# Key normalisation as one reciprocal on one side, the triangular inverse tied to its data, and a new order of lanes in the RWKV-7 stage of a hybrid decoder layer

## The chip, the cores and the metric

The kernel is one program for one core of a Trainium2 chip. The metric is device time of one execution in microseconds (us), the median of several executions. "Before" is the kernel without the change, "after" the kernel with it.

## The reference

One layer of a hybrid decoder on an input of 1 x 1024 x 1024 in float32: norm, one combined input projection, an RWKV-7 branch and an S5 branch side by side, gates, a merge, an output projection, and a gated convolutional FFN. What the change touches is the RWKV-7 branch, with 8 heads of 64 channels over 1024 positions:

```python
kk = (k * k_k).reshape(hs)
kk = kk / jnp.maximum(jnp.linalg.norm(kk, axis=-1, keepdims=True), 1e-12)
k = k * (1.0 + (a - 1.0) * k_a)
...
y = wkv7_scan(rh, decay.reshape(hs), kh, vh, -kk, kk * ah)

def step(S, inp):                      # in wkv7_scan, over the positions
    r_t, w_t, k_t, v_t, a_t, b_t = inp
    sa = jnp.einsum('bhij,bhj->bhi', S, a_t)
    S = (S * w_t[:, :, None, :] + sa[..., None] * b_t[:, :, None, :]
         + v_t[..., None] * k_t[:, :, None, :])
    return S, jnp.einsum('bhij,bhj->bhi', S, r_t)
```

Here a_t is -kk and b_t is kk times a, both with the normalised key. In the state's update they occur only as a product, an a of one position with a b of another of the same head. Behind the scan each head's output is normalised (mean and variance over 64 channels), scaled, and a bonus is added.

## The kernel before

All large products are fp32 made of three products of split operands (L172 to L174, high by high, high by low, low by high; each 128x512). Their results go to PSUM, an activation or an add takes them out, and ACT and DVE split weights and data into halves (L156, L157). TensorE is in use nearly throughout.

The RWKV stage is cut into four units i = 0..3: a group of four heads (i%2) on half of the sequence (i//2). Each unit has two halves u = 0, 1 of two heads each, 128 channels on the partitions and 512 positions on the free axis. A unit goes through these steps:

- **Front** (`rwkv_front`, once per u). Loads key, rate and decay (tiles `ld`), squares the key on ACT (L668), sums it per head on PE (L672), which gives 8 sums per partition, and takes the inverse root with eleven small DVE instructions (`rsqrt`, L136 to L141, 128x8 each, or 128x8 in integers). The decay goes through a running sum (L679, DVE) and two exponentials (L681, L682, ACT). The inverse norm is spread over 512 columns (L687, ACT, into a part of `gr`) and transposed on PE into `kb` (L689), after which four 512-wide DVE instructions (L690, L691, L693, L694) make the a side `ar` and the b side `bk`. GpSimd (POOL) makes the other halves (L665, L666, L678, L692, L695, L696) and copies the last decay of each chunk into `pt` (L683). Then come the Gram products of 64 positions (L706) with masks on DVE (L709) into `gr`, their store to DRAM (`md`, L714), and the bonus (L718).
- **Inverse** (`rwkv_inv`). The 32x32 unit triangular blocks of `gr` come back from `md` in another layout (`mt`, L756). The solution `x` starts as the identity (L757, an ACT copy of a constant), and 31 steps of two DVE instructions (L763, L765) eliminate row after row. `x` goes to DRAM (`xd`, L768) and back into `gr` (L775). POOL issues all these transfers.
- **Nat** (`rwkv_nat`, per u). Transposes of `bk` (L736), their copies `bkn` on ACT (L739), transposes of v (L745) and a copy to `V` (L747).
- **Level** (`rwkv_level`). DVE transposes the inverted blocks (L787, into a tile of the `ld` ring), small products join two blocks to 64 (L794, L802).
- **Chain** (`rwkv_chain`): 8 chunks in sequence, each L835 (state times a), a copy `p` and two scalings `spt` = S by `pt` (L840) on ACT, L844, a copy `U` on DVE (L846), L852 and L854, and the new state S (L856, DVE). `chain_v` (L817 to L821) is the part that needs no state.
- **Out** (`rwkv_out`): the norm of `yn` on DVE (L869 to L879), transposes of the result on PE (L885), scale (L887), two additions (L892), and a store.

**What sets the order.** The order of PE's instructions is written out by `drive`. It runs lanes, which are Python generators. A lane yields a cost and a delay: the cost is added to a virtual clock, and the lane may go on once the clock has passed the delay. At each point the first lane in the list that is ready goes on. When none is, or when the lanes have used up a credit, a piece of background work (the large gate, merge and projection products) is placed. So the constants T_... decide how many large products stand between a step and its successor, and the list decides who goes first. The other engines' instructions are ordered by a scheduler from priorities and its own simulation; each engine then runs strictly in its order. `prep_lane(u)` holds front and inverse, `chain_lane` nat, level, chain and out. The front of unit i+1 may start when nat of unit i is done.

Of the kernel before, what the change touches and what calls it, by code (L numbers as in the profile page):

```python
# [9 lines left out]
F32 = mybir.dt.float32  # L10
# [61 lines left out]
class Kern:  # L72
# [572 lines left out]
    def rwkv_front(self, d, u):  # L645
# [11 lines left out]
        def c64(x):  # L657
            return x.rearrange("p (c t) -> p c t", t=64)
# [15 lines left out]
        sv = self.small.tile([128, 8], F32, tag="sv", name=self.nm("sv"), bufs=2)  # L674
        V.tensor_scalar(sv, st.rearrange("p a b -> p (a b)"), 1e-24, None, ALU.max)
        y = self.rsqrt(sv, 8, "pr")

        G.tensor_scalar(tz, tz, 1.0, 1.0, ALU.add, ALU.mult)  # L678
# [4 lines left out]
        G.tensor_copy(d["pt"][:, :, u], pe[:, :, 64])  # L683
# [6 lines left out]
        V.scalar_tensor_tensor(kk, k, self.vec("k_k", p), kb, ALU.mult, ALU.mult)  # L690
        V.scalar_tensor_tensor(ar0, c64(kk), -1.0, pe[:, :, 0:64], ALU.mult, ALU.mult)  # L691
        G.tensor_tensor(ar1, c64(r), pe[:, :, 1:65], ALU.mult)  # L692
        V.scalar_tensor_tensor(kk, ta, 1.0, kk, ALU.add, ALU.mult)  # L693
        V.scalar_tensor_tensor(bk0, c64(kk), 0.5, c64(tz), ALU.mult, ALU.mult)  # L694
# [29 lines left out]
    def rwkv_nat(self, d):  # L724
# [6 lines left out]
        for u in range(2):  # L731
# [8 lines left out]
            yield 1.0, 0.3  # L740
# [6 lines left out]
            A.copy(d["V"][:, :, u], ps)  # L747
            yield 1.0, 0.8

    def rwkv_inv(self, d):  # L750
# [6 lines left out]
        A.copy(x, self.cst("xinit").rearrange("p (s t) -> p s t", t=32).unsqueeze(1).to_broadcast([128, 2, 8, 32]))  # L757
        mt = mt.rearrange("p u (q t) -> p u q t", t=32)
        for q in range(31):
# [17 lines left out]
    def rwkv_level(self, d):  # L777
# [5 lines left out]
        xz = self.tg("ld", NLD).rearrange("p (u c t) -> p u c t", u=2, t=32)  # L783
# [78 lines left out]
    def rwkv_out(self, d):  # L862
# [17 lines left out]
        yield 0, T_LN  # L880
# [813 lines left out]
    def front_half(self):  # L1694
# [35 lines left out]
        with tc.tile_pool(name="rk", bufs=1) as self.rk, tc.tile_pool(name="evb", bufs=NEV) as self.evp, \  # L1730
# [4 lines left out]
            self.nat = self.prep = -1  # L1735
# [33 lines left out]
    def chain_lane(self, mg):  # L1769
        for i, d in enumerate(self.ds):  # L1770
# [20 lines left out]
T_LD, T_LT = 9.0, 3.0  # L1791
NEVA = 4
T_KN, T_BK, T_GR, T_INV, T_LV, T_CH, T_LN = 5.0, 9.0, 2.5, 36.0, 1.0, 0.8, 11.0
# [87 lines left out]
```

## Time and profile before

| | us |
|---|---|
| median of 3 runs | 1615.97 |
| lowest and highest run | 1611.21, 1623.19 |
| profiled execution, whole | 1613.51 |
| its span in the trace | 1611.7 |
| PE busy in the span | 1508.9 (94%) |
| mean granted TensorE clock | 0.962 of full speed |

The span is the time from the first to the last instruction of the profiled execution; the remaining 1.8 us lie around it. The RWKV stage takes about 285 to 715 us of it. "Clock" is the share of full TensorE speed that was granted: a stretch of 6 us with a clock of 0.50 ran at half speed throughout.

### The profile page before, as it was taken

The numbers are of one execution on the slowest core, as the hardware profiler recorded it, in microseconds if no ns is written. First come the engines' busy times: TensorE is split into PE (matmuls) and PEld (weight loads), VectorE is DVE, ScalarE is ACT, GpSimd is POOL, SyncE is SP. The second block draws the span as 40 slices with busy tenths as digits, with TensorE's granted clock in tenths as the row PEclk, the third lists the DMA queues.
The fourth block names the chain that finished last, engine by engine and source line by source line (L and its number), as shares of the span: only waits on it lengthen the run. The fifth ranks groups of instructions, "written<-read, shape, count | busy, mean of one in ns | idle before, by whom it ended". The sixth has DMA issues, their size and how long they took to land. (4 is left out here: it accounts for less than half of the span.)

```text
span 1611.7 us, 26125 instructions
## 1 busy us (share of the span) xinstructions
PE 1508.9 (94%) x10028; PEld 1207.6 (75%) x10028; DVE 1126.7 (70%) x2039; ACT 696.8 (43%) x1109; POOL 155.0 (10%) x226
## 2 busy tenths in 40 slices
PE   5899899898999999889998999999999999999995
PEld 4688787686776776667866888788888887788784
DVE  5798774565365555865668579977777776788677
ACT  4345552224233344554443445554444444443451
POOL 2100001314123142010000000000000000000000
PEclk9799999999999999989988999999999999999997
DMA  5244334243352353552574453322222224963622
GB/s 178 63 140 142 98 113 169 65 136 117 106 153 94 97 171 107 171 156 93 190 223 156 144 190 125 124 79 83 90 89 78 78 87 142 321 215 106 229 84 104
DMA packets 133420, 213.84 MB, mean 133 GB/s; under 512 B 38656, under 2 KB 44800, under 8 KB 133296
## 3 DMA queue, kind: packets, MB, share of 16 engines
q1 hardware_dynamic: 124208, 188.32, 35.5%
q0 software_dynamic: 7936, 21.77, 4.6%
q10 hardware_dynamic: 1152, 2.10, 0.3%
q8 instruction: 78, 1.28, 0.3%
q14 instruction: 46, 0.38, 0.1%
HBM read 156.56 MB, written 53.48 MB: 130 GB/s over the span
## 5 line engine op out<-in xcount | busy, mean ns | idle before, releaser
L172 PE MATMUL gm<-hh,wh 128*128 128x512 f32 x688 | 299.6, 436 | 6.5 <-ACT hh L226 3.3
L173 PE MATMUL gm<-hl,wh 128*128 128x512 f32 x688 | 279.1, 406 | 5.4 <-DVE hl L227 4.5
L174 PE MATMUL gm<-hh,wl 128*128 128x512 f32 x688 | 276.6, 402 | 0.0
L156 ACT CAST wh<-wf 128x512 fp32r<-128x512 f32 x179 | 110.7, 620 | 196.7 <-PE gm L173 108.5
L157 DVE TENSOR_TENSOR wl<-wf,wh 128x512 fp32r<-128x512 f32 x179 | 124.8, 698 | 100.7 <-ACT wh L156 97.5
L172 PEld LDWEIGHTS gm<-hh,wh 128*128 128x128 f32 x688 | 134.0, 195 | 45.2 <-ACT hh L226 5.6
L173 PEld LDWEIGHTS gm<-hl,wh 128*128 128x128 f32 x688 | 134.2, 195 | 32.4 <-DVE hl L227 7.3
L174 PEld LDWEIGHTS gm<-hh,wl 128*128 128x128 f32 x688 | 134.1, 195 | 30.0
L1504 PE MATMUL d<-xl,wh 128*128 128x512 f32 x308 | 121.1, 393 | 3.3 <-DVE xl L227 3.3
L1503 PE MATMUL d<-xh,wh 128*128 128x512 f32 x308 | 120.8, 392 | 2.1 <-ACT xh L226 2.1
L1505 PE MATMUL d<-xh,wl 128*128 128x512 f32 x308 | 120.5, 391 | 0.0
L1329 PE MATMUL rp<-t,h 128*128 128x512 f32 x216 | 84.4, 391 | 1.9 <-ACT p L1343 1.9
L1331 PE MATMUL rp<-t,l 128*128 128x512 f32 x216 | 84.2, 390 | 0.5 <-DVE l L227 0.5
L1330 PE MATMUL rp<-t,h 128*128 128x512 f32 x216 | 84.1, 389 | 0.0
L1504 PEld LDWEIGHTS d<-xl,wh 128*128 128x128 f32 x308 | 58.1, 189 | 16.8 <-DVE xl L227 4.9
L1503 PEld LDWEIGHTS d<-xh,wh 128*128 128x128 f32 x308 | 58.2, 189 | 14.7 <-ACT xh L226 2.5
L1505 PEld LDWEIGHTS d<-xh,wl 128*128 128x128 f32 x308 | 58.2, 189 | 12.2
L226 ACT CAST h<-r 128x1024 fp32r<-128x1024 f32 x34 | 35.8, 1054 | 61.4 <-PE rp L1330 29.6
L227 DVE TENSOR_TENSOR l<-r,h 128x1024 fp32r<-128x1024 f32 x34 | 41.6, 1225 | 29.5 <-ACT h L226 28.0
L1350 DVE SCALAR_TENSOR_TENSOR y<-zv,vecs,y 128x1023 f32<-128x1023 f32 (+1 forms) x36 | 46.1, 1280 | 8.6 <-ACT y L1348 8.6
L1329 PEld LDWEIGHTS rp<-t,h 128*128 128x128 f32 x216 | 40.5, 188 | 11.4 <-ACT p L1343 2.7
L1331 PEld LDWEIGHTS rp<-t,l 128*128 128x128 f32 x216 | 40.5, 188 | 9.3 <-DVE l L227 1.0
(437 smaller groups left out, 3364.1 us busy)
## 6 DMA issues: line engine op xcount, KB each, us to landing
r<-in_w_up_dram SPq DMA_DIRECT2D x36, 512.0 KB, 3.2
wf<-in_w_in_dram SPq DMA_DIRECT2D x68, 256.0 KB, 2.9
st<-in_w_down_dram SPq DMA_DIRECT2D x55, 256.0 KB, 4.3
st<-ACT SPq DMA_DIRECT2D x44, 256.0 KB, 4.4
wf<-in_w_up_dram SPq DMA_DIRECT2D x36, 256.0 KB, 2.8
ACT<-y POOLq DMA_DIRECT2D x18, 512.0 KB, 2.9
GT<-ev SPq DMA_DIRECT2D x32, 256.0 KB, 2.3
wf<-in_w_br_dram SPq DMA_DIRECT2D x32, 256.0 KB, 3.1
```

The costliest lines, as they stand in the source:

```text
L156: nc.scalar.copy(h[:, :n], f[:, :n])
L157: nc.vector.tensor_tensor(l[:, :n], f[:, :n], h[:, :n].bitcast(F32), ALU.subtract)
L172: mm(ps, a, xh[k], start=k == 0, stop=False)
L173: mm(ps, a, xl[k], start=False, stop=False)
L174: mm(ps, b, xh[k], start=False, stop=k == n - 1)
L1329: mm(ps, wh[:, c], xh, start=first and k == 0, stop=False, skip_group_check=True)
L1330: mm(ps, wh[:, c], xl, start=False, stop=False, skip_group_check=True)
L1331: mm(ps, wl[:, c], xh, start=False, stop=k == 3, skip_group_check=True)
L1350: V.scalar_tensor_tensor(y[:, lag:], z[:, 0:1024 - lag], self.vec(nme, i), y[:, lag:], ALU.mult, ALU.add)
L1503: mm(ps, wh[:, c], xh[:, x], start=start, stop=False, skip_group_check=True)
L1504: mm(ps, wh[:, c], xl[:, x], start=False, stop=False, skip_group_check=True)
L1505: mm(ps, wl[:, c], xh[:, x], start=False, stop=stop, skip_group_check=True)
```

## The change

- **Norm on one side.** The root is gone. `sv` is the sum, bounded below, and one reciprocal of it (128x8) goes to the b side alone; the a side gets key by `k_k` by decay without a norm. Since a and b are only ever multiplied with each other within a head, this needs the reciprocal of the squared norm that belongs to b's position; the a side's own norm is carried by nothing else. Three of the four 512-wide DVE instructions now stand ahead of the reciprocal, and only one, the last product of the b side, needs `kb`.
- **Small moves.** The addition of 1 to the decay's tanh moves from POOL in the front to POOL in the input stage, ahead of that tile's store. The `pt` copy moves from POOL to ACT.
- **Inverse.** The ACT copy of the constant is gone. The first elimination step (row 0, whose multiplier is the constant's first column) is folded with it into three DVE instructions: two products of 128x256 and one addition of 128x512. They read `mt`, so `x` is not written before `mt` is there. The other 30 steps stay.
- **Level's tile.** The tile for the transposed blocks is taken in nat, and a copy of two columns from nat's last PSUM tile into it (ACT) ties the DVE transposes behind nat.
- **Lanes.** The front lanes stand ahead of the chain in the list. Out is a lane of its own at the end of the list, and chain i waits until out i-1 has been placed.
- **Constants.** T_NT (nat's gap between the transposes of `bk` and of v) 0.3 to 1.5, T_BK (front, ahead of the Gram products) 9 to 6, T_LT 3 to 4, T_INV 36 to 41, T_LN (out, ahead of its transposes) 11 to 18, but 11 (T_LE) for the last unit.

```diff
@@ rwkv_front
-        sv = self.small.tile([128, 8], F32, tag="sv", name=self.nm("sv"), bufs=2)
-        V.tensor_scalar(sv, st.rearrange("p a b -> p (a b)"), 1e-24, None, ALU.max)
-        y = self.rsqrt(sv, 8, "pr")
-
-        G.tensor_scalar(tz, tz, 1.0, 1.0, ALU.add, ALU.mult)
+        y = self.small.tile([128, 8], F32, tag="sv", name=self.nm("sv"), bufs=2)
+        V.tensor_scalar(y, st.rearrange("p a b -> p (a b)"), 1e-24, None, ALU.max)
+        V.reciprocal(y, y)
+
         V.tensor_tensor_scan(tz, self.cst("smask"), tz, 0.0, ALU.mult, ALU.add)
         G.memset(pe[:, :, 0:1], 1.0)
         A.activation(pe[:, :, 1:65], c64(tz), AF.Exp, scale=-0.5 * CDEC)
         A.activation(tz, tz, AF.Exp, scale=0.5 * CDEC)
-        G.tensor_copy(d["pt"][:, :, u], pe[:, :, 64])
+        A.copy(d["pt"][:, :, u], pe[:, :, 64])
+        V.scalar_tensor_tensor(bk0, c64(ta), 1.0, c64(k), ALU.add, ALU.mult)
+        V.scalar_tensor_tensor(ar0, c64(k), self.vec("k_k", p), pe[:, :, 0:64], ALU.mult, ALU.mult)
+        V.scalar_tensor_tensor(bk0, bk0, self.vec("k_k", p), c64(tz), ALU.mult, ALU.mult)
...
-        V.scalar_tensor_tensor(kk, k, self.vec("k_k", p), kb, ALU.mult, ALU.mult)
-        V.scalar_tensor_tensor(ar0, c64(kk), -1.0, pe[:, :, 0:64], ALU.mult, ALU.mult)
+        V.scalar_tensor_tensor(bk0, bk0, -0.5, c64(kb), ALU.mult, ALU.mult)
         G.tensor_tensor(ar1, c64(r), pe[:, :, 1:65], ALU.mult)
-        V.scalar_tensor_tensor(kk, ta, 1.0, kk, ALU.add, ALU.mult)
-        V.scalar_tensor_tensor(bk0, c64(kk), 0.5, c64(tz), ALU.mult, ALU.mult)
@@ rwkv_nat
-            yield 1.0, 0.3
+            yield 1.0, T_NT
...
+            if u:
+                d["xz"] = self.tg("ld", NLD).rearrange("p (u c t) -> p u c t", u=2, t=32)
+                A.copy(d["xz"][:, :, 0, 0:1], ps[:, 0:2, 0:1])
@@ rwkv_inv
-        A.copy(x, self.cst("xinit").rearrange("p (s t) -> p s t", t=32).unsqueeze(1).to_broadcast([128, 2, 8, 32]))
-        for q in range(31):
+        xi = self.cst("xinit").rearrange("p (s t) -> p s t", t=32)
+        for u in range(2):
+            V.tensor_tensor(x[:, u], xi[:, :, 0:1].to_broadcast([128, 8, 32]), mt[:, u, 0:1].to_broadcast([128, 8, 32]), ALU.mult)
+        V.tensor_tensor(x, x, xi.unsqueeze(1).to_broadcast([128, 2, 8, 32]), ALU.add)
+        for q in range(1, 31):
@@ rwkv_level
-        xz = self.tg("ld", NLD).rearrange("p (u c t) -> p u c t", u=2, t=32)
+        xz = d["xz"]
@@ rwkv_out
-        yield 0, T_LN
+        yield 0, latency
@@ lowrank
+                    if dst is self.TZ:
+                        nc.gpsimd.tensor_scalar(t, t, 1.0, 1.0, ALU.add, ALU.mult)
                     nc.sync.dma_start(dst[p][:, th * 512:th * 512 + 512], t)
@@ the stage, chain_lane
-            self.drive([(HP2, self.chain_lane(mg)), (HP, self.prep_lane(0)), (HP, self.prep_lane(1))])
+            self.drive([(HP, self.prep_lane(0)), (HP, self.prep_lane(1)), (HP2, self.chain_lane()), (HP2, self.out_lane(mg))])
...
+            yield 0, lambda: self.outs >= i
             yield from self.rwkv_chain(d)
             if i == 3:
                 self.pause, self.chained = False, True
-            yield from self.rwkv_out(d)
+            self.chains = i
+
+    def out_lane(self, mg):
+        for i, d in enumerate(self.ds):
+            yield 0, lambda: self.chains >= i
+            yield from self.rwkv_out(d, T_LN if i < 3 else T_LE)
             self.outs += 1
@@ constants
-T_KN, T_BK, T_GR, T_INV, T_LV, T_CH, T_LN = 5.0, 9.0, 2.5, 36.0, 1.0, 0.8, 11.0
+T_KN, T_BK, T_GR, T_INV, T_LV, T_CH = 5.0, 6.0, 2.5, 41.0, 1.0, 0.8
+T_NT, T_LN, T_LE = 1.5, 18.0, 11.0
```

**What moves on the engines.** Three places show it. The first is ACT in nat of unit 0, before and then after. L739 (L738 after) are the copies `bkn`, L747 (L746) the copies `V`, L757 the preset of the inverse's `x`, L749 after the two-column copy, L1021 a gate's activation.

```order
L739 COPY bkn_3239<-rp_3242 128x8x64
L747 COPY V_3240<-rp_3280 128x8x64
L757 COPY x_4070<-csts 128x512
L739 COPY bkn_3239<-rp_3304 128x8x64
L739 COPY bkn_3239<-rp_3305 128x8x64
```

```order
L738 COPY bkn_3232<-rp_3235 128x8x64
L1021 ACTIVATE ev_3297<-gm_3216,hb_b_gate 128x512
L746 COPY V_3233<-rp_3279 128x8x64
L738 COPY bkn_3232<-rp_3307 128x8x64
L738 COPY bkn_3232<-rp_3308 128x8x64
L156 CAST wh_3662<-wf_3664 128x512
L746 COPY V_3233<-rp_3352 128x8x64
L749 COPY ld_3370<-rp_3352 128x2
```

The preset of unit 1 (x_4070) stood ahead of the second pair of `bkn` copies of unit 0; now there is none on ACT, and the two-column copy stands behind the last `V` copy.

The second is PE at the same step, before and then after: the last transposes of `bk` (L736, L735), background products (gm), and the transposes of v (L745, L744).

```order
L736 MATMUL rp_667_3305<-csts_201,bk_524_2472 64x64
L172 MATMUL gm_660_3235<-hh_39_321,wh_657_3229 128x512
L173 MATMUL gm_660_3235<-hl_40_322,wh_657_3229 128x512
L174 MATMUL gm_660_3235<-hh_39_321,wl_658_3230 128x512
L745 MATMUL rp_668_3343<-csts_201,ld_566_2684 64x64 x16
```

```order
L735 MATMUL rp_664_3308<-csts_201,bk_524_2480 64x64
L172 MATMUL gm_662_3300<-hh_88_494,wh_649_3204 128x512
L173 MATMUL gm_662_3300<-hl_89_495,wh_649_3204 128x512
L174 MATMUL gm_662_3300<-hh_88_494,wl_650_3205 128x512
L172 MATMUL gm_662_3300<-hh_90_499,wh_649_3204 128x512
L173 MATMUL gm_662_3300<-hl_91_500,wh_649_3204 128x512
L174 MATMUL gm_662_3300<-hh_90_499,wl_650_3205 128x512
L172 MATMUL gm_662_3300<-hh_92_504,wh_652_3210 128x512
L173 MATMUL gm_662_3300<-hl_93_505,wh_652_3210 128x512
L174 MATMUL gm_662_3300<-hh_92_504,wl_653_3211 128x512
L744 MATMUL rp_665_3352<-csts_201,ld_562_2666 64x64 x16
```

Three large products stood between the two groups, now nine.

The third is DVE at the norm of unit 0's front, before and then after. bk and ar are the b and a side, sv the sums, L679 (L678 after) the running sum of the decay, L157 the split of a weight; before, the rows of `rsqrt` (L136 and on) go on beyond the last row shown.

```order
L679 SCALAR_TENSOR_TENSOR ld_2490<-csts,ld_2490 128x512
L943 SCALAR_TENSOR_TENSOR ev_2537<-gm_2512,vecs,ev_2537 128x511
L945 COPY last<-gm_2512 128x1
L157 TENSOR_TENSOR wl_2731<-wf_2732,wh_2730 128x512
L675 TENSOR_SCALAR sv_2566<-rp_2561 128x8
L675 TENSOR_SCALAR sv_2594<-rp_2589 128x8
L136 TENSOR_SCALAR rsy_2568<-sv_2566 128x8
L136 TENSOR_SCALAR rsy_2596<-sv_2594 128x8
```

```order
L683 SCALAR_TENSOR_TENSOR bk_2480<-ld_2496,ld_2494 128x8x64
L678 SCALAR_TENSOR_TENSOR ld_2498<-csts,ld_2498 128x512
L684 SCALAR_TENSOR_TENSOR ar_2479<-ld_2485,vecs,gr_2481 128x8x64
L948 SCALAR_TENSOR_TENSOR ev_2545<-gm_2520,vecs,ev_2545 128x511
L950 COPY last<-gm_2520 128x1
L684 SCALAR_TENSOR_TENSOR ar_2479<-ld_2494,vecs,gr_2481 128x8x64
L685 SCALAR_TENSOR_TENSOR bk_2480<-bk_2480,vecs,ld_2489 128x8x64
L157 TENSOR_TENSOR wl_2773<-wf_2774,wh_2772 128x512
L675 TENSOR_SCALAR sv_2574<-rp_2569 128x8
L675 TENSOR_SCALAR sv_2592<-rp_2587 128x8
L676 RECIPROCAL sv_2574<-sv_2574 128x8
L676 RECIPROCAL sv_2592<-sv_2592 128x8
```

The a and b products now stand ahead of the sums `sv`, and where eleven small instructions per half followed them, one reciprocal does. The numbers of PE's rows are the same (6708), DVE has 1903 rows where it had 1976, and PE's order is the same up to row 860 and from row 3495 on. The order also shows, without rows here, where the lanes put their steps on PE: between the last bonus product (L718, L717 after) and the first L794 (L799) of units 0 to 3 stood 201, 162, 162 and 162 products of 128x512 and now stand 240, 174, 177 and 174, with 104 more small products of the chain for the last three; and between the last product of a chain and its out transposes stood 57 products of 128x512 for every unit, where for units 1 and 2 now stand 66, with 64 small transposes of nat and other small products, and for the last still 57.

More of the change, by code (lines that the diff above doesn't have):

```diff
@@ L860, in rwkv_chain, with rwkv_out @@
             yield 0.6, T_CH, 2.0
-    def rwkv_out(self, d):
+    def rwkv_out(self, d, latency):
         th = d["th"]
@@ L1734, in front_half @@
             self.ds = [{} for _ in range(4)]
-            self.nat = self.prep = -1
+            self.nat = self.prep = self.chains = -1
             self.fronts = 0
             mg, self.mx0 = [], []
-            self.drive([(HP2, self.chain_lane(mg)), (HP, self.prep_lane(0)), (HP, self.prep_lane(1))])
+            self.drive([(HP, self.prep_lane(0)), (HP, self.prep_lane(1)), (HP2, self.chain_lane()), (HP2, self.out_lane(mg))])
             self.drain(lambda: self.mark)
@@ L1767, in prep_lane, with chain_lane @@
                 self.prep = i
-    def chain_lane(self, mg):
+    def chain_lane(self):
         for i, d in enumerate(self.ds):
@@ L1790 @@
 T_US, T_TAB0, T_TAB, T_TRIG, T_SCAN = 5.0, 38.0, 20.0, 12.0, 13.0
-T_LD, T_LT = 9.0, 3.0
+T_LD, T_LT = 9.0, 4.0
 NEVA = 4
-T_KN, T_BK, T_GR, T_INV, T_LV, T_CH, T_LN = 5.0, 9.0, 2.5, 36.0, 1.0, 0.8, 11.0
+T_KN, T_BK, T_GR, T_INV, T_LV, T_CH = 5.0, 6.0, 2.5, 41.0, 1.0, 0.8
+T_NT, T_LN, T_LE = 1.5, 18.0, 11.0
 T_X = 3.0
```

## Prediction

> **What bounds the kernel now.** I read the busy table first, to see which engine sets the span.
>
> ```profile
> span 1611.7 us, 26125 instructions
> PE 1508.9 (94%) x10028; PEld 1207.6 (75%) x10028; DVE 1126.7 (70%) x2039; ACT 696.8 (43%) x1109; POOL 155.0 (10%) x226
> ```
>
> PE is busy for 1508.9 of 1611.7 us. The number of PE's instructions does not change, so a gain can only come from PE's idle time and from its clock, and only in the RWKV stage, since PE's order is the same before and behind it. Next the stage as one window (columns: length, then busy time and count of PE, PEld, DVE, ACT and POOL, the clock, DMA share, GB/s), and PE's waits in it.
>
> ```profile
> 285.00:715.00 430.00, 396.26 (x4557) 296.93 (x4556) 250.27 (x674) 161.49 (x341) 112.13 (x157) 0.95 0.43 126
> PE cz L794 <- DVE ld L787: 11.4, 12, 2.8
> PE rp L689 <- ACT gr L687: 9.4, 2, 5.6
> PE rp L885 <- DVE yn L879: 6.3, 1, 6.3
> PE rp L745 <- ACT bkn L739: 3.3, 1, 3.3
> PE cz L844 <- ACT p L837: 1.5, 1, 1.5
> PE rp L706 <- DVE gr L709: 0.9, 1, 0.9
> ```
>
> PE is idle for 430.00 - 396.26 = 33.7 us, and these six rows hold 32.8 of it. Asked in short windows, the first two split up in time: units 1, 2 and 3 wait for their inverted blocks, and unit 3 for its `kb`; the 5.6 us of the second row are unit 0's.
>
> ```profile
> PE cz L794 <- DVE ld L787: 4.9, 4, 2.0
> PE cz L794 <- DVE ld L787: 2.1, 4, 1.1
> PE rp L689 <- ACT gr L687: 3.7, 1, 3.7
> PE cz L794 <- DVE ld L787: 4.5, 4, 2.8
> ```
>
> These are the windows 477 to 487, 583 to 590, 603 to 610 and 701 to 710 us. A wait costs more than itself if the clock falls behind it, so I took 6 us right behind each of the seven longest waits.
>
> ```profile
> 296.90:302.90 6.00, 6.00 (x21) 5.13 (x22) 3.30 (x5) 1.06 (x2) 0.00 (x0) 0.61 0.14 54
> 369.90:375.90 6.00, 6.00 (x67) 4.90 (x68) 1.71 (x4) 1.80 (x4) 5.96 (x10) 0.72 0.21 47
> 485.30:491.30 6.00, 5.96 (x74) 4.64 (x74) 2.45 (x2) 3.88 (x8) 4.71 (x6) 0.67 0.33 114
> 588.40:594.40 6.00, 5.83 (x55) 4.30 (x57) 0.48 (x2) 1.62 (x4) 2.72 (x4) 0.50 1.00 332
> 608.30:614.30 6.00, 6.00 (x51) 4.38 (x52) 4.38 (x12) 2.52 (x7) 0.00 (x0) 0.72 0.26 88
> 684.40:690.40 6.00, 6.00 (x83) 5.14 (x84) 5.72 (x17) 2.34 (x4) 0.00 (x0) 0.76 0.39 140
> 708.60:714.60 6.00, 5.81 (x55) 4.28 (x57) 2.65 (x4) 3.52 (x6) 0.00 (x0) 0.50 0.73 174
> ```
>
> PE works throughout these windows, at clocks of 0.50 to 0.76. Six us at a clock of 0.61 do 3.66 us of work, so 2.3 us are lost; in order the losses are 2.3, 1.7, 2.0, 3.0, 1.7, 1.4 and 3.0, in sum 15.1 us. Idle and clock together make 32.8 + 15.1 = 47.9 us, the most that this change can take away.
>
> **The change part by part.** I go through the waits in the order of time.
>
> *Unit 0's front (5.6 + 0.9 idle, 2.3 clock).* The ACT timeline, then the DVE timeline, show how its wait comes about.
>
> ```profile
> 289.85 0.35 ACT L840 ACTIVATE spt<-S,pt 128x64 f32<-128x64 f32 x1 [3.27 <-POOL pt L683]
> ...
> 296.19 1.14 ACT L687 COPY gr<-rsy 128x512 f32<-128x512 f32 x2 [4.37 <-DVE rsy L141]
> 291.53 0.23 DVE L675 TENSOR_SCALAR sv<-rp 128x8 f32<-128x8 f32 x2
> 291.72 1.11 DVE L136 TENSOR_SCALAR rsy<-sv 128x8 int32<-128x8 int32 x2
> ...
> 295.99 0.28 DVE L141 SCALAR_TENSOR_TENSOR rsy<-rsh,rsy 128x8 f32<-128x8 f32 x2
> ```
>
> ACT sat 3.27 us in front of a scaling that needed POOL's `pt`, with the weight cast and thereby DVE's queue behind it; `sv` ran only at 291.53. Then the root took until 296.27 for both halves, 4.5 us behind `sv`. Both go: `pt` is now ACT's own copy, and a reciprocal takes the root's place. The trace has none; from below I bound it by `sv` itself (0.23 us for two) and from above by L136's pair (1.11), and take 0.3 since it is one instruction of the same 128x8 floats as `sv`. So 4.2 us of chain and 3.3 us of queue go against a wait of 5.6. Against it, the a and b products now stand ahead of `sv` in DVE's queue. Their price is in these groups.
>
> ```profile
> L679 DVE TENSOR_TENSOR_SCAN ld<-csts,ld 128x512 f32<-128x512 f32 x6 | 10.0, 1674 | 11.1 <-POOL ld L678 11.1
> L691 DVE SCALAR_TENSOR_TENSOR ar<-gr 128x512 f32<-128x512 f32 x8 | 5.4, 687 | 0.1
> L681 ACT ACTIVATE gr<-ld 128x512 f32<-128x512 f32 x7 | 4.4, 630 | 6.2 <-DVE ld L679 6.2
> L687 ACT COPY gr<-rsy 128x512 f32<-128x512 f32 x8 | 4.8, 615 | 16.8 <-DVE rsy L141 16.8
> ```
>
> For two halves these are 2 x (1.67 + 3 x 0.69) = 7.5 us from the loads' landing, against scans and root, 2 x 1.67 + 4.5 = 7.8, before. The running sum no longer waits for POOL (11.1 us of idle in its row), so they start earlier. For unit 0, I count 8.0 of 8.8 us as gone.
>
> *Unit 0's nat (3.3 idle, 1.7 clock) and L844 (1.5).* ACT again.
>
> ```profile
> 368.70 0.62 ACT L757 COPY x<-csts 128x512 f32<-128x512 f32 x1 [5.09 <-DMA xd<-x]
> 369.23 1.07 ACT L739 COPY bkn<-rp 128x512 f32<-128x512 f32 x2
> ```
>
> The preset of unit 1's `x` waited 5.09 us for the store of unit 0's `x`, and the `bkn` copies, with PE behind them, waited in ACT's queue. With the preset off ACT this goes whole. On DVE the new preset waits for the same tile and for `mt`, and what is queued there behind it are U copies and S updates of the chain; but `mt` lands only behind the front's stores to `md`, and the scheduler can set other work ahead. The inverse pays nothing: two instructions of a step go and three come. L844's wait sits in the same stretch of a queue that the front's copies fill; I count it. Sum 6.5.
>
> *The inverted blocks of units 1, 2 and 3.* The cover between bonus and L794 grows by 12, 15 and 12 products of 128x512 and by 104 small ones, less eight transposes. What one costs:
>
> ```profile
> 677.20 0.39 PE L172 MATMUL gm<-hh,wh 128*128 128x512 f32 x1
> 677.42 0.39 PE L173 MATMUL gm<-hl,wh 128*128 128x512 f32 x1
> 396.59 0.46 PE L835 MATMUL cz<-S,ar 64*64 64x64 f32 x16
> 396.98 0.50 PE L172 MATMUL gm<-hh,wh 128*128 128x512 f32 x1
> ```
>
> A large one takes 0.22 us from start to start, sixteen small ones 0.39. So 2.6 to 3.3 us come from the large and 2.5 from the small, some 5 to 6, and up to 9 if every change of shape costs 0.1. That is as much as the waits of units 1 and 2 (4.9 and 2.1 us), so both go with their clock: 6.9 + 5.1 = 12.0.
>
> *Out of unit 2 (6.3 idle, 1.4 clock) and the blocks of unit 3 (4.5, 3.0).* These two are not independent. The cover of out grows from 57 large products (12.8 us) to 66 and at least 100 small ones (17.3 or more). The need was 12.8 + 6.3 = 19.1. So most of it goes, but the 7.7 us lay inside the stretch in which unit 3's inverse ran, and hid that much of it.
>
> ```profile
> 678.00:688.00 10.00, 3.66 (x15) 3.31 (x15) 9.83 (x30) 4.27 (x7) 0.00 (x0) 0.66 0.66 209
> L763 DVE TENSOR_TENSOR tm<-x,mt x31: 180/270/318, 659.5 to 695.0; 128x120 f32<-128x120 f32 x3, 128x56 f32<-128x56 f32 x2, 128x108 f32<-128x108 f32 x2, 128x96 f32<-128x96 f32 x2
> ```
>
> DVE is full there (9.83 of 10 us), and the steps took from 659.5 to 695.0. If out no longer stalls, the blocks are needed 7.7 us earlier, and the cover gives 5 to 9. So of 15.2 us together I take 8.0.
>
> *Unit 3's `kb` (3.7 idle, 1.7 clock).* The root goes (4.2 us), but the products that now stand ahead of `sv` wait for the decay's exponentials, and additions of an out lie among them in the order. I take 3.0 of 5.4.
>
> *What is new.* The fronts of units 1 to 3 come ahead of the chain, with 21 to 24 large products (4.7 to 5.3 us) as cover between L672 and `kb`, where units 1 to 3 had 25 to 34 (5.7 to 7.6, an estimate from the same start-to-start). Their four Gram groups stand closer together; the wait for L709 was 0.9 us where two groups followed each other. Chain steps get queued behind the front's products on DVE, 0.69 us at a time. The decay's stores wait for POOL's addition (0.6 us) in the input stage, where PE has other products. I charge 2 us for each of three fronts, from between nothing (7.5 against 7.8 us of chain) and 5.4 (what unit 3's `kb` cost), and 1 us for the rest: 7.
>
> One rule of the Trainium skill speaks against my clock terms. "TensorE: Matmul & The Clock Gate", in "What's actually happening", has the clock halved after an idle window of about 3.4 us. By it the waits of units 1 to 3 on their blocks, four pieces of at most 2.8 us each, cost no clock, and the most to be had is 47.9 - 8.0 = 39.9. The trace disagrees: behind 2.1 us of waits in pieces the clock was 0.50 for 6 us, so I keep the 3.0.
>
> The sum: 8.0 + 6.5 + 12.0 + 8.0 + 3.0 - 7 = 30.5 us. From the profiled execution's 1613.5 us that leaves 1583. Its time lies 2.5 us under the median of the runs shown, so the forecast for the median is 1616.0 - 30.5 = 1585.
>
> **The rivals.** *The reciprocal is late (0.13).* On DVE, `sv` now follows eight large instructions that need loads, a running sum and ACT's exponentials; if one of them waits, `kb` is late in every front. Four fronts at 3.7 us and 1.7 clock, as unit 3's before, are 21.6 us in place of the 7 that I charged, and a gain of 30.5 + 7 - 21.6 = 16 us is left, or 7 if the Gram groups wait 3 us in three fronts too: 1600 to 1609. For it: 7.5 against 7.8 us is no margin. Against: the running sum waits no more for POOL.
>
> *DVE still sets the inverse (0.15).* In units 1 to 3 the blocks come late by as much as PE gains ahead of them: the 12.0 and the 8.0 shrink to half, 10 us less, 1595, still inside the forecast's own gain of 20 to 42. For it: DVE's 9.83 of 10. Against: PE had no wait between bonus and blocks of units 1 and 2.
>
> *Slower: POOL and DVE hold each other up (0.09).* The a and b products now run on DVE beside POOL's large ones.
>
> ```profile
> L692 POOL TENSOR_TENSOR ar<-ld,gr x8: 1175/1191/2145, 283.6 to 603.0; 128x512 f32<-128x512 f32 x8
> ```
>
> One L692 took 2145 ns against a median of 1191. If each of POOL's five large instructions per half and front takes 0.95 us longer, a front's Gram products come 2 x 5 x 0.95 = 9.5 us later, plus 3 us of clock, 50 us for four fronts, of which nat, chain and inverse behind them hide nothing since they wait for the same front. That is 30.5 + 7 - 50 = 12 us slower, 1628. It decides from 37.5 us of new waits on, 9.4 a front. For it, the trace's slow L692; against, seven of eight took the short time, and the same number of DVE instructions ran beside POOL's before. "GPSIMD Engine Reference", section "Specifications", says that GpSimd shares its SBUF interfaces with VectorE and contends with DVE instructions of two SBUF inputs, which the new products are; by that, the 2145 would be the rule.
>
> *More than forecast (0.08):* all 47.9 us and no new wait, 1568. *The order does not come out as the lanes intend (0.03):* within 5 us of before.
>
> **How the numbers follow.** The forecast (gain of 20 to 42 us, 0.52) gives the time, 1585. The low end is everything gone, 1568, less 1 for the spread of the runs; the high end takes in the late reciprocal nearly whole, 1608. Below the low end lies about 0.03, above the high end the slower rival, the unchanged case and a quarter of the late reciprocal, 0.15. One per cent is 16 us, about what a measurement of this kernel tells from no change. Faster by over 1%: 0.52 + 0.08 + 0.15, and 0.02 of the late reciprocal, 0.77. Within 1%: the rest of it, 0.11, and the unchanged case, 0.03, make 0.14. Slower: 0.09.
>
> **What would show it.** PE's waits in the stage, 33.7 us, should fall below 14, with no row for L745 and L885, and L794 under 5 us. The stage's clock should rise from 0.95 to 0.98. ACT should have no COPY of `x` and no wait for POOL's `pt`, and the row of the `kb` transposes should stay under 8 us. The prediction is wrong if that row, or the Gram products' wait for the b side, is above 15 us; if L794's wait is as large as before, DVE's inverse was the limit; and if POOL's rows mean over 2 us each, the slower rival holds.

## The result, and the profile after

| | before | after | ratio, 95% interval |
|---|---|---|---|
| median of 18 runs, us | 1615.55 | 1604.26 | 0.9933 (0.9919 to 0.9947) |
| lowest and highest, us | 1611.21, 1623.19 | 1596.32, 1611.32 | |
| profiled execution, us | 1613.51 | 1611.32 | |

The change makes the kernel 11.3 us faster, 0.7%: inside the forecast's range, but a bit over a third of the forecast gain of 30.5 us, and in the case "within 1%" that had a chance of 0.14. The profiled execution is as slow as the slowest of the 18, so it is read below by stretches and not by its sum.

The busy table of after, then its RWKV stage as one window (columns as in the prediction):

```profile
span 1609.0 us, 26071 instructions
PE 1513.4 (94%) x10028; PEld 1198.9 (75%) x10028; DVE 1132.1 (70%) x1963; ACT 695.5 (43%) x1117; POOL 169.6 (11%) x218
```

```profile
285.00:715.00 430.00, 406.32 (x4822) 300.04 (x4820) 256.90 (x608) 166.47 (x373) 116.57 (x145) 0.98 0.42 128
```

In 430 us of the stage PE is idle for 23.7 us where it was 33.7, at a clock of 0.98 where it was 0.95, and gets through 4822 instructions where it did 4557. Yet over the whole span PE is busy for 4.5 us longer than before with the same 10028 instructions. PE's waits in the stage of after:

```profile
PE cz L799 <- DVE ld L792: 5.0, 3, 3.6
PE rp L717 <- DVE gr L708: 4.2, 1, 4.2
PE cz L849 <- ACT p L842: 3.3, 1, 3.3
PE rp L691 <- ACT gr L689: 2.5, 3, 1.2
PE rp L705 <- DVE gr L708: 2.1, 5, 0.8
PE cz L857 <- DVE U L851: 1.5, 1, 1.5
PE rp L744 <- ACT bkn L738: 1.4, 2, 1.2
```

L794 is L799 now, L689 is L691, L745 is L744, L885 is L890, L844 is L849, and L706 is L705. The wait for out (6.3 us) is gone, that for `kb` is 2.5 us instead of 9.4, that for the blocks 5.0 instead of 11.4, and that for `bkn` 1.4 instead of 3.3. The Gram products wait 2.1 us instead of 0.9, the chain for its `p` 3.3 instead of 1.5, and 4.2 us of the bonus product behind the masks are new. PE is thus idle for 9.7 us more than the 14 us that the prediction named as its sign. The 4.2 us and the 3.3 us come from unit 3 and have one cause, which ACT's timeline of after shows:

```profile
598.98 1.28 ACT L1057 ACT_TABLE_LOAD   x1 [11.69 <-DMA ld<-YU]
600.27 1.15 ACT L1057 ACTIVATE ld<-ld 128x512 f32<-128x512 f32 x2
601.32 0.60 ACT L156 CAST wh<-wf 128x512 fp32r<-128x512 f32 x1
...
619.07 0.63 ACT L1057 ACTIVATE ld<-ld 128x512 f32<-128x512 f32 x1 [8.87 <-DMA ld<-YU]
...
620.75 0.24 ACT L842 COPY p<-cz 128x128 f32<-128x128 f32 x1
```

L1057 is the activation of S5's output, which the merge loads (YU). ACT stood in front of it for 11.69 and 8.87 us. The weight cast behind it held DVE's split and, in DVE's queue, the masks (L708), as DVE's timeline shows:

```profile
601.96 0.69 DVE L157 TENSOR_TENSOR wl<-wf,wh 128x512 fp32r<-128x512 f32 x1 [6.40 <-ACT wh L156]
602.57 1.28 DVE L708 TENSOR_TENSOR gr<-rp,csts 128x512 f32<-128x512 f32 x2
```

The copy `p` stood behind the second activation. In after ACT reached the first of them at 587.3 us, and its load was issued only at 595.1. In before ACT stood in front of the same four loads for only 2.3 us, in three pieces.

Another loss is not in the stage. Here is the same stretch of 200 us far behind it, from before and then from after, in which PE's order is the same in both:

```profile
1100.00:1300.00 200.00, 200.00 (x884) 165.59 (x883) 150.66 (x166) 97.40 (x116) 5.33 (x10) 1.00 0.23 84
```

```profile
1100.00:1300.00 200.00, 200.00 (x863) 162.09 (x861) 150.34 (x166) 97.00 (x113) 5.33 (x10) 1.00 0.23 82
```

PE never rests in either, and the clock is 1.00 in both. But 884 products begin in before and 863 in after: 0.2262 us against 0.2317 each, 2.4% more for the same work. The table shows what that does; it holds the start (us) of PE's n-th instruction in the traces, counted from 0, in whose order n = 1250 stands at the stage's begin, 6500 behind it, and 7250 to 9000 in the FFN.

| n | before | after | difference |
|---|---|---|---|
| 1250 | 286.2 | 286.8 | +0.6 |
| 6500 | 776.6 | 763.3 | -13.3 |
| 7250 | 957.4 | 944.5 | -12.9 |
| 9000 | 1354.4 | 1350.4 | -4.0 |

13.9 us are gained from 1250 to 6500, and 8.9 are given back between 7250 and 9000, where nothing waits.

### The profile page after: what moved, and what is told of

It reads as the page before. It is cut to its first block, busy times and chain, and to the rows that moved or that the text cites. A ratio compares the mean times of both kernels' runs of the same rounds, so it can differ in the third digit from the quotient of the medians.

```text
span 1609.0 us, 26071 instructions
## 1 busy us (share of the span) xinstructions
PE 1513.4 (94%) x10028; PEld 1198.9 (75%) x10028; DVE 1132.1 (70%) x1963; ACT 695.5 (43%) x1117; POOL 169.6 (11%) x218
## 3 DMA queue, kind: packets, MB, share of 16 engines
q1 hardware_dynamic: 124208, 188.32, 35.9%
## 4 chain that ended last, share of the span: by engine, by line
PE 53%; DVE 11%; DMA 9%; issue 4%; ACT 3%; SPq 1%; POOL 0%; DVEq 0%; ACTq 0%; POOLq 0%
PE gm L172 6%; PE gm L173 4%; PE gm L174 4%; PE rp L1336 4%; PE rp L1338 4%; PE rp L1337 4%; DMA st<-in_w_down_dram 2%; PE mm L1338 2%; PE mm L1337 2%; PE mm L1336 2%; PE ch L172 2%; PE ch L173 1%; PE ch L174 1%; PE mm L173 1%; PE d L1511 1%
## 5 line engine op out<-in xcount | busy, mean ns | idle before, releaser
L172 PE MATMUL gm<-hh,wh 128*128 128x512 f32 x688 | 297.4, 432 | 7.0 <-ACT hh L226 4.2
L174 PE MATMUL gm<-hh,wl 128*128 128x512 f32 x688 | 276.2, 402 | 0.0
L157 DVE TENSOR_TENSOR wl<-wf,wh 128x512 fp32r<-128x512 f32 x179 | 127.1, 711 | 106.4 <-ACT wh L156 101.0
L172 PEld LDWEIGHTS gm<-hh,wh 128*128 128x128 f32 x688 | 132.3, 192 | 45.3 <-ACT hh L226 6.2
L174 PEld LDWEIGHTS gm<-hh,wl 128*128 128x128 f32 x688 | 132.8, 193 | 31.0
L227 DVE TENSOR_TENSOR l<-r,h 128x1024 fp32r<-128x1024 f32 x34 | 41.7, 1226 | 30.5 <-ACT h L226 29.1
L1350 ACT COPY p<-rp 128x512 f32<-128x512 f32 x54 | 31.4, 581 | 40.9 <-PE rp L1338 39.1
```

Source lines behind the costliest of these rows:

```text
L157: nc.vector.tensor_tensor(l[:, :n], f[:, :n], h[:, :n].bitcast(F32), ALU.subtract)
L172: mm(ps, a, xh[k], start=k == 0, stop=False)
L174: mm(ps, b, xh[k], start=False, stop=k == n - 1)
```

## The experiments

The first four take the change apart and try the merge's loads. The times are ratios to the kernel before.

**The preset alone.**

```diff
-        A.copy(x, self.cst("xinit").rearrange("p (s t) -> p s t", t=32).unsqueeze(1).to_broadcast([128, 2, 8, 32]))
-        for q in range(31):
+        xi = self.cst("xinit").rearrange("p (s t) -> p s t", t=32)
...
+        V.tensor_tensor(x, x, xi.unsqueeze(1).to_broadcast([128, 2, 8, 32]), ALU.add)
+        for q in range(1, 31):
```

> The kernel before with only the inverse's preset changed (products on DVE that read the loaded blocks, 30 steps instead of 31, no copy on ACT). By my sum the wait of the v transposes for the copies of the b side (3.3 us) and its slow clock (1.7 us) go, all else stays: PE's idle time in the stage 33.7 to about 30 us, 5 us less in all, 0.997. Rival: the preset's wait for the loaded blocks now stands on DVE ahead of the chain's copies and updates, and the 5 us come back there as waits for U or S: 1.000.

Measured: 1.0036 (1.0011 to 1.0061). PE's waits in the stage:

```profile
PE cz L797 <- DVE ld L790: 19.9, 11, 6.7
PE rp L888 <- DVE yn L882: 6.2, 1, 6.2
PE rp L689 <- ACT gr L687: 5.4, 2, 4.6
```

The wait of nat's v transposes is gone, as expected of the first theory, but the wait for the blocks went from 11.4 to 19.9 us. It is not the chain that pays, as the rival had it, but the inverse: from the last bonus product to the landing of the blocks it took 62.1, 61.7 and 71.5 us for units 1 to 3, where before it took 60.5, 57.2 and 67.6. The step "the inverse pays nothing" was wrong.

**The norm alone.**

```diff
-        y = self.rsqrt(sv, 8, "pr")
...
+        V.reciprocal(y, y)
...
+        A.copy(d["pt"][:, :, u], pe[:, :, 64])
...
+        V.scalar_tensor_tensor(bk0, bk0, -0.5, c64(kb), ALU.mult, ALU.mult)
```

> The kernel before with only the key's norm changed (reciprocal on the b side, products ahead of it, the addition of 1 moved to the input stage, the copy of the last decay on ACT). By my sum unit 0's front gains 8 us and unit 3's wait for kb (3.7 us and 1.7 us of clock) shrinks by 3 or more: 11 us less, 0.993, and no wait of the kb transposes above 1.5 us. Rival (the reciprocal is late behind the products): the row of the kb transposes stays at 9 us or grows, 1.000 or slower.

Measured: 1.0045 (1.0019 to 1.0070). The waits of PE in its stage, and the stretch behind it:

```profile
PE cz L793 <- DVE ld L786: 12.4, 8, 3.2
PE rp L884 <- DVE yn L878: 6.1, 1, 6.1
PE rp L744 <- ACT bkn L738: 3.9, 1, 3.9
PE cz L843 <- ACT p L836: 3.5, 3, 1.5
```

```profile
1100.00:1300.00 200.00, 200.00 (x862) 162.07 (x862) 147.51 (x163) 95.92 (x112) 5.33 (x10) 1.00 0.24 82
```

No wait for `kb` is left in the list, where 9.4 us stood, so the reciprocal is not late. The kernel is slower all the same, and has 862 products in the 200 us. The wide spacing comes with this part.

**The order alone.**

```diff
+            self.drive([(HP, self.prep_lane(0)), (HP, self.prep_lane(1)), (HP2, self.chain_lane()), (HP2, self.out_lane(mg))])
...
+                A.copy(d["xz"][:, :, 0, 0:1], ps[:, 0:2, 0:1])
...
+T_NT, T_LN, T_LE = 1.5, 18.0, 11.0
```

> The kernel before with only the order changed (front lanes first, out as its own lane, the level's tile tied to nat, all the constants). By my sum the waits for unit 1's and 2's blocks and for unit 2's out go, 12 + 8 us with their clock, less 7 us of new waits: 13 us less, 0.992. If the loads of S5's output for the merge, which now fall into unit 3's front, are what ate the gain, the activation behind them waits 10 us or more on ACT here too, with 7 us of PE's idle time and 4 us of clock behind it, and only about 2 to 5 us are gained, 0.998.

Measured: 0.9987 (0.9967 to 1.0007). Its 200 us hold 884 products. ACT's waits in it between 560 and 660 us:

```profile
ACT L1053 <- DMA ld<-YU: 13.2, 1, 13.2
ACT yn L862 <- PE cz L857: 9.7, 4, 3.7
ACT ld L1053 <- DMA ld<-YU: 9.5, 1, 9.5
```

ACT stands in front of the merge's loads here too, and the gain is small and not clear of none, as the second case of the expectation said. In this run the wait for `kb` is still there (10.6 us), so the merge is not its only loss. The three parts do not add up to the whole: 1.0036, 1.0045 and 0.9987 make 1.007, the change has 0.9933. That the longer cover of the order hides the longer inverse, and the shorter front fits the order, is my reading; no run tests it.

**The change with the merge tied to unit 3's Gram.**

```diff
-                y = self.s5_y(self.tg("ld", NLD, s8), b, 0)
+                t = self.tg("ld", NLD, s8)
+                nc.scalar.copy(t[:, 0, 0:2], self.ds[3]["gr"][:, 1, 7, 1, 126:128])
+                y = self.s5_y(t, b, 0)
```

> The changed kernel, with the merge's four S5 tiles written first with two columns of unit 3's last Gram result, so that their loads and the activation on ACT come behind unit 3's Gram products. If ACT's waits of 11.7 and 8.9 us for these loads are what ate the gain, PE's waits of 4.2 us (bonus behind the masks) and 3.3 us (the chain's p) go with their half clock, some 11 us less than the changed kernel: 0.986 of before. If the gain went to something else (the spacing of the products, 0.232 us in the profiled run against 0.227 before), the waits may go but the time stays: 0.993.

Measured: 0.9934 (0.9909 to 0.9958), the time of the change. The wait behind the masks is gone, but waits of 3.5 us for S and 2.8 us for `p` stand in the list, and the 200 us hold 862 products. From the 4750th to the 5000th of PE's instructions, where the loads fall, this run takes 23.9 us and the change 32.5; from there to the 6500th it takes 140.9 and the change 135.7. So the tie takes the loss away where it stood and makes a new one behind it. The next four runs ask first where the spacing comes from. The change removes the root's two pairs of small tiles, 2 x 2 x 8 floats or 128 bytes per partition, and the built programs show what that moves in SBUF (byte addresses of the first weight tile and the first data tile, and their rest modulo 256):

```
                     weights wh        data hh
before               25920 (64)        196416 (64)
after                25792 (192)       196416 (64)
```

**The change with 128 unused bytes** in the pool that had the root's tiles.

```diff
+        nc.gpsimd.memset(self.small.tile([128, 32], F32, tag="fill", name="fill", bufs=1), 0.0)
```

> The changed kernel with one unused tile of 32 floats per partition in the pool of small tiles, which has as many bytes (128) as the two pairs of small tiles of the root that the change removed; all else is the same. If the products are spaced at 0.232 us instead of 0.227 because every later tile in SBUF has moved by 128 bytes, the spacing comes back to 0.227 outside the stage and the kernel gains some 1.1 to 1.5% on the changed one: 0.980 to 0.983 of before. If the spacing comes from something else (the instructions, a fuller PE), it stays at 0.232 and the time at 0.993.

Measured: 0.9871 (0.9840 to 0.9901), 1594.44 us. The stretch behind the stage, and the stage:

```profile
1100.00:1300.00 200.00, 200.00 (x884) 165.58 (x884) 153.91 (x169) 98.17 (x117) 5.31 (x10) 1.00 0.23 85
...
285.00:715.00 430.00, 411.70 (x4932) 305.33 (x4932) 258.02 (x619) 169.16 (x377) 114.88 (x144) 0.98 0.43 130
```

884 products again, and 0.6% of the kernel is back. From the 7250th to the 9000th instruction PE takes 396.9 us, before 397.0, after 405.9. The gain was below the 1.1 to 1.5% that I had expected of it.

**The kernel before with the same 128 bytes.**

```diff
+        nc.gpsimd.memset(self.small.tile([128, 32], F32, tag="fill", name="fill", bufs=1), 0.0)
```

> The kernel before with the same unused tile of 128 bytes and no other change. If SBUF addresses alone set the spacing, it changes from 0.227 here too, to 0.231 or 0.232 in the parts where PE has large products, and the kernel gets 1 to 1.5% slower, 1.010 to 1.015; if only a shift the other way does it, or it is something else, 1.000.

Measured: 1.0075 (1.0046 to 1.0104). The 200 us of this run:

```profile
1100.00:1300.00 200.00, 200.00 (x862) 162.14 (x861) 150.31 (x166) 97.01 (x114) 5.32 (x10) 1.00 0.22 82
```

A tile that nothing uses makes the kernel 12 us slower, less than the 1 to 1.5% that I had expected.

**The norm alone with the 128 bytes.**

```diff
+        nc.gpsimd.memset(self.small.tile([128, 32], F32, tag="fill", name="fill", bufs=1), 0.0)
```

> The key's norm alone (as in the run of the norm only) with the unused tile. If its 1.0045 was the shift, it comes down by 1.1 to 1.5%, to 0.990 to 0.993, which is the 8 to 11 us that my sum gave for this part; if the reciprocal itself was late, it stays above 1.000.

Measured: 0.9971 (0.9951 to 0.9991), 884 products. Without the shift the norm gains about 5 us, half of what my sum gave it: its `kb` waits go, but the waits for the blocks (12.9 us) and for `p` (3.4 us) grew by 3.4 us together. Fronts that end earlier need their later steps earlier; that this is the reason is not shown.

**The tied merge with the 128 bytes.**

```diff
+        nc.gpsimd.memset(self.small.tile([128, 32], F32, tag="fill", name="fill", bufs=1), 0.0)
```

> The changed kernel with the merge's S5 tiles tied to unit 3's Gram result and the unused tile. Against the changed kernel with the unused tile alone this shows what ACT's waits for the merge's loads cost: 8 to 11 us less (0.974 of before) if they are on PE's path, the same if they are not.

Measured: 0.9872 (0.9838 to 0.9906), the same as without the tie. ACT's waits between 575 and 640 us show why:

```profile
ACT wh L156 <- PE gm L173: 10.3, 4, 6.8
ACT yn L864 <- PE cz L859: 7.7, 4, 3.1
ACT ev L1021 <- PE gm L174: 6.2, 2, 3.7
ACT ld L1057 <- DMA ld<-YU: 4.5, 1, 4.5
```

The third load was issued at 599.01 and landed at 606.85 us, beside the reload of unit 3's blocks in many small packets; ACT still stood 4.5 us in front of it, and PE 3.0 us for `p` behind it. The first two loads were cured and the third took over. The stretch from the 4750th to the 5000th instruction takes 27.3 us, without the tie 31.3, but the one behind it, to the 6500th, 139.2 where it took 134.7. So the last four runs ask which addresses count, and whether a later tie holds.

**The change with the data moved as well**, by a larger filler at the other end of SBUF.

```diff
-                self.nc.gpsimd.memset(pad.tile([128, 40], F32, name="pad"), 0.0)
+                self.nc.gpsimd.memset(pad.tile([128, 72], F32, name="pad"), 0.0)
```

> The changed kernel with the filler at the other end of SBUF made 32 floats larger, so that the tiles with the data (which the products stream) move by 128 bytes as the weights' tiles did. If only the distance of the two counts (both are 192 above a multiple of 256 bytes then, before both 64), the spacing is 0.227 and the time that of the changed kernel with the unused tile, 0.985 to 0.989; if the weights' own address counts, the spacing stays at 0.232 and the time at 0.993.

Measured: 0.9849 (0.9833 to 0.9865), 1591.29 us. The 200 us of this run:

```profile
1100.00:1300.00 200.00, 200.00 (x884) 165.62 (x883) 153.61 (x169) 98.18 (x117) 5.32 (x10) 1.00 0.23 85
```

Weights (25792) and data (196288) are now both at a rest of 192, and the spacing is back. So neither address alone sets it; it is the distance of the two that counts.

**The kernel before with 256 unused bytes.**

```diff
+        nc.gpsimd.memset(self.small.tile([128, 64], F32, tag="fill", name="fill", bufs=1), 0.0)
```

> The kernel before with 256 unused bytes in place of 128. If the distance of weights and data modulo 256 bytes sets the spacing, nothing changes: 0.227 and 1.000. If every shift from the tuned place costs, 1.0075 as with 128 bytes.

Measured: 0.9980 (0.9964 to 0.9996). The 200 us of this run:

```profile
1100.00:1300.00 200.00, 200.00 (x884) 165.62 (x883) 153.06 (x169) 97.91 (x117) 5.32 (x10) 1.00 0.23 85
```

A shift by 256 bytes costs nothing; that it came out 0.2% faster stays unexplained.

**The 128 bytes and the merge tied to unit 3's reloaded blocks.**

```diff
...
+                t = self.tg("ld", NLD, s8)
+                nc.scalar.copy(t[:, 0, 0:2], self.ds[3]["mt"][:, 1, 1022:1024])
```

> The changed kernel with the unused tile and with the merge's four S5 tiles tied to unit 3's reloaded blocks (mt), so that their loads do not run beside the many small transfers of these blocks. If ACT standing in wait for these loads is what unit 3 still loses, the waits of 3.6 us for the masks and of 3.5 us for the chain's p go with two half-clock episodes and nothing takes their place: 7 to 10 us less than with the unused tile alone, 0.981 to 0.983. If the loads then come too late for the merge, a wait of the large products for the splits of S5's output takes their place: 0.987 or more.

Measured: 0.9813 (0.9799 to 0.9826), 1586.92 us, the fastest of all. PE's waits in the stage:

```profile
PE cz L799 <- DVE ld L792: 5.3, 3, 3.9
PE rp L705 <- DVE gr L708: 2.1, 5, 0.8
PE cz L840 <- DVE S L861: 1.9, 3, 1.2
PE rp L691 <- ACT gr L689: 1.7, 2, 1.3
PE rp L744 <- ACT bkn L738: 1.4, 2, 1.3
PE cz L849 <- ACT p L842: 1.3, 1, 1.3
```

No wait behind the masks, and none for YU on ACT. Against the 128 bytes alone it gains 0.6%, against the run with the data moved 0.36%, 6 to 9 us in all. Where it gains shows in the 250 instructions of PE from the 4750th on, which are the same in both but for the order of eight small ones; here first with the 128 bytes alone, then with the tie:

```profile
587.10:618.40 31.30, 24.22 (x251) 16.20 (x250) 8.88 (x19) 11.45 (x27) 7.91 (x14) 0.89 0.56 135
592.80:613.70 20.90, 20.90 (x251) 14.40 (x250) 8.82 (x19) 8.77 (x23) 7.90 (x14) 1.00 0.57 153
```

Without the tie PE is idle for 7.1 us and loses 3.4 us to the clock (11% of 31.3); with it PE never rests, at full clock. That is 10.4 us, and 3.5 us come back up to the 6500th instruction (138.2 against 134.7). The whole stretch from the 1250th to the 6500th differs by only 1.8 us (465.9 against 467.7), because this execution was 5.1 us slower ahead of the 4750th, where the tie has nothing to move. With the data moved the same 250 instructions took 27.0 us: there ACT stood in front of the later load for 6.0 us instead of 9.1, and PE's wait for `p` was 0.4 us.

**The 128 bytes and the old preset.**

```diff
+        A.copy(x, self.cst("xinit").rearrange("p (s t) -> p s t", t=32).unsqueeze(1).to_broadcast([128, 2, 8, 32]))
...
-        V.tensor_tensor(x, x, xi.unsqueeze(1).to_broadcast([128, 2, 8, 32]), ALU.add)
-        for q in range(1, 31):
+        for q in range(31):
```

> The changed kernel with the unused tile and the inverse's preset as before (a copy on ACT, 31 steps). By my sum the copy stands in front of the b side's copies again and 5 us come back, 0.990. If the preset on DVE costs the inverse as much as it saves nat (as the run of the preset only suggests), the time stays, 0.987, or falls where the longer cover hides nothing of it.

Measured: 0.9862 (0.9847 to 0.9877). PE's wait for the `bkn` copies, whose cause in before was the preset on ACT, in this run:

```profile
PE rp L744 <- ACT bkn L738: 1.4, 2, 1.3
```

The wait does not return with the copy on ACT. In the order alone, with the old preset too, this row is 1.2 us. So the new order removes the wait; that it does so by the nine products that now cover the copies where three did fits, but was not tried alone. Within what these runs tell apart, the new preset is worth nothing in the changed kernel.

## Why the prediction came out as it did

**The bound.** This is the step that failed: "a gain can only come from PE's idle time and from its clock, and only in the RWKV stage, since PE's order is the same before and behind it". The order is the same, but the price of a product is not. Removing the root's small tiles moved the tiles behind them, the weights' among them, by 128 bytes against the data, and nearly all large products outside the middle of the stage, up to some 1360 us, came 2.4% further apart. This term of the sum, put at nothing, is priced by pairs of runs that differ in this alone: 0.6% (after, with and without the fill), 0.74% (the norm), 0.75% (before) and 0.84% (after, with the data moved), or 10 to 14 us of the 19.2 us that the forecast missed. A second term put at nothing, the loads of the merge, is below. The code held a warning: it has a filler tile at one end of SBUF, and the diff removes tiles from a pool that lies ahead of others.

**Unit 0's front.** Right: no wait of L691 or L705 above 0.8 us is left in it. The reciprocal took 195 ns (median of 8), two of them 0.32 us, where I took 0.3.

**Nat and its preset.** Right in the time (L744's rows 1.4 instead of 3.3 us), but only half right in the cause. In the old order the preset on ACT does make the wait, since the preset alone removes it; but the new order removes it too, with the old preset in place. And "the inverse pays nothing" was wrong: the new preset alone makes it 2 to 5 us longer.

**The blocks and out.** The waits of units 1 and 2 and of out are gone, as forecast. That of unit 3 is 5.0 us with a slow clock behind it; I had kept 7 us of it and of out together. But my reason, that DVE still sets the inverse there, was wrong. The steps of unit 3's inverse took 26.7 us in after (from 629.7 to 656.4), 35.9 before, and its blocks landed at 669.3. What PE waits for is the transposes' place in DVE's queue, in after's timeline:

```profile
677.08 2.04 DVE L1063 TENSOR_TENSOR e<-et,e 128x512 fp32r<-128x512 f32 x2 [3.74 <-ACT e L1062]
...
680.06 1.04 DVE L1063 TENSOR_TENSOR e<-et,e 128x512 fp32r<-128x512 f32 x1 [0.29 <-ACT e L1062]
681.01 0.89 DVE L792 STREAM_TRANSPOSE ld<-gr 32x256 f32<-32x256 f32 x2
```

They stand behind splits of the merge that wait for ACT. No run moves these splits, so this is read from the trace and not shown by an experiment.

**Unit 3's `kb`.** Better than forecast: no wait of L691 is left in unit 3's front, where I had kept 2.4 of 5.4 us. The 2.5 us of that row belong to units 1 and 2.

**What is new.** I charged 7 us for fronts and Gram groups. The rows that this meant (L691, L705 and the small waits of the chain) hold 2.5 + 2.1 + 1.5 us in after, so the charge was right for them; but the 4.2 and 3.3 us behind the merge's loads, with their slow clock, were missing. Two 6 us windows behind them in after show it:

```profile
603.40:609.40 6.00, 6.00 (x28) 3.13 (x28) 2.25 (x5) 2.20 (x6) 4.59 (x9) 0.60 0.51 122
621.10:627.10 6.00, 6.00 (x72) 4.25 (x76) 2.81 (x7) 3.55 (x9) 0.00 (x0) 0.72 0.31 89
```

That is 7.5 us of idle time and 2.4 + 1.7 us of clock, 11.6 in all. The tie to the reloaded blocks, in the kernel with the 128 bytes, confirms the size: it took 10.4 us off the same stretch, of which 3.5 came back behind it. The list of what is new names the queues that a step of the stage is moved past, but not the merge, which is no part of the diff and comes only with the end of out 1.

With the addresses restored and the merge moved out of the way the change gains 30.2 us by the ratio of 0.9813, against a forecast of 30.5. This agreement is partly luck: in the two traces only 24.5 us of it lie in the stage (from the 1250th to the 6500th instruction 465.9 against 490.4 us), where the forecast put all of its gain, and unit 3's blocks still cost 5.3 us.

**The rivals.** The late reciprocal did not happen. POOL and DVE do hold each other up, as the slower rival said, but not by the 37.5 us from which it decides. My argument against it was wrong: in before, none of the a and b products ran beside a POOL instruction other than the issue of a transfer. POOL's rows, for which a mean of over 2 us was to be the sign, have means of 1.46 to 1.89 us. Three lines by their tiles, two of after and one of before, as minimum, median and maximum in ns:

```profile
L685 DVE SCALAR_TENSOR_TENSOR bk<-bk,vecs,ld x8: 736/1481/1777, 285.6 to 574.5; 128x512 f32<-128x512 f32 x8
L684 DVE SCALAR_TENSOR_TENSOR ar<-ld,vecs,gr x8: 721/1588/1806, 283.0 to 571.7; 128x512 f32<-128x512 f32 x8
```

```profile
L691 DVE SCALAR_TENSOR_TENSOR ar<-gr x8: 681/686/693, 299.5 to 615.0; 128x512 f32<-128x512 f32 x8
```

The price of 0.69 us for these was half of what they took, 1.5 us. PE's wait for `kb` is 2.5 us all the same. That the earlier place of these products hides the rest is my reading; no run tests it.

## What to carry to other kernels

A change that adds or removes a tile in a pool that others lie behind has a price of its own. Compare a stretch that the edit does not touch, by the count of products in a window at full clock, before reading anything into the sum, and restore the old places with an unused tile to see the edit itself. A step that comes earlier also meets what is loaded and activated there for a later stage: look through each in-order queue for instructions of stages that the diff does not name.

## What the runs showed of the hardware

**Products depend on where weights and data lie.** With weights and data a multiple of 256 bytes apart in SBUF, products of 128x512 start every 0.2262 us; 128 bytes further, every 0.2317. Kernels of the first kind at three different places (before, before with 256 bytes, after with the data moved) hold 884 in 200 us, and four of the second kind (after, the norm alone, before with 128 bytes, the tied merge) 862 or 863. Within the one trace of after, the products of L172 to L174 say the same, with the addresses from the built program: 2451 pairs of neighbours with a rest of 64 for the data and of 192 for the weights start 232 ns apart in the median, 226 pairs with 192 for both 227. Other distances than 128 were not tried. Nor is it known why the products in the middle of the RWKV stage, from 400 to 715 us, are 232 to 235 ns apart in the median in all kernels, before among them.

**DVE beside POOL.** L684 and L685 read two tiles from SBUF and a scalar for each partition. They took 0.74 us with POOL idle, 0.72 us beside POOL's L665, which reads one tile, and 1.0 to 1.8 us beside POOL's products of two tiles (L666, L693, L694, L695). L692, which reads one of its two from PSUM, took 0.67 to 0.69 us whether POOL was busy or not. That agrees with "GPSIMD Engine Reference" of the Trainium skill, "Specifications", which names contention with DVE instructions of two SBUF inputs; the size is the trace's.

**The clock falls after short waits, too.** In before, 2.1 us of waits in four pieces, the longest 1.1 us, were followed by a clock of 0.50 over 6 us. The pieces lie between products of 32x32 (L794); these alone do not do it, since the same products of after's units 1 and 2, without a wait, were followed by a clock of 1.00:

```profile
472.00:478.00 6.00, 6.00 (x65) 4.98 (x64) 5.78 (x6) 5.43 (x11) 5.83 (x4) 1.00 0.52 188
```

A rule by which it takes an idle window of about 3.4 us ("TensorE: Matmul & The Clock Gate" of the Trainium skill, "What's actually happening") would have cleared the four pieces, and the trace disagrees. Behind after's one wait of 3.3 us for `p` the clock was 0.72 over 6 us, which is too near to 3.4 to tell.
